# Prompt attention moved in among the steps of the sample attention, in one hybrid decoder layer

## The chip, the cores and the metric

The kernel runs on one core of a Trainium2 chip. The metric is device microseconds (us) of one execution, as the median of several runs. TensorE (PE) does the matrix products and the transposes, VectorE (DVE) and ScalarE (ACT) the elementwise work and the copies out of PSUM, GpSimd (POOL) some elementwise work and the indirect loads, SyncE (SP) issues most loads. Every engine works through its own instructions in the order in which they were written.

## What is computed

One decoder layer runs on 1024 prompt tokens and on 64 sample tokens (8 sequences of 8 tokens, each with 4096 cached tokens in pages of 128). Two feed-forward blocks stand around a middle part: an input projection, then attention over a latent of 256 numbers per token (8 heads, plus a rotated key of 32 numbers) beside a causal depthwise convolution of width 31, then one output projection over both. Cut to the two attentions:

```python
def attend_prompt(q_abs, q_pe, c_kv, k_pe):          # causal, blocks of 128 queries
    s = (einsum('bthc,bsc->bhts', qa_b, c_kv) + einsum('bthr,bsr->bhts', qp_b, k_pe)) * SM_SCALE
    p = softmax(where(qpos[:, None] >= kpos[None, :], s, NEG_INF))
    return einsum('bhts,bsc->bthc', p, c_kv)

def attend_sample(q_abs, q_pe, c_kv, k_pe, cache_kv, cache_kr, page_table):
    c_past, r_past = cache_kv[page_table], cache_kr[page_table]     # 4096 cached tokens
    s = concatenate([scores against the cache, causal scores against the 8 new tokens])
    p = softmax(s)
    return p_past @ c_past + p_new @ c_kv

attn_out = einsum('bthc,chv->bthv', o_lat, w_uv)
x = x + concatenate([rms_norm(attn_out), rms_norm(conv_out)]) @ w_out
```

## The kernel before

The kernel writes its own instruction order. `Flow` (`fl`) is a planner with a clock of its own: `fl.spend(ns)` lets that many planned nanoseconds pass, and side jobs (the convolution, norms, delayed stores) are written out when they fall due. A generator that yields `None` has nothing to write now.

**Sample attention** is `mgen`, 32 steps of 1024 cached tokens. A step (`qk`, `trans`, `expo`, `pv`) forms scores from eight cached key pages (`kst` tiles of two pages, six tiles ahead, `KBUF`), evicts them on DVE into `Ssb`, takes exponentials, transposes 4 blocks, and five or six steps later multiplies them with the cached values (`cst` tiles, seven ahead, `CBUF`). `load_k` reads the key pages: three tiles in four through SP, with a page number loaded into a register first, and every fourth tile as an indirect load of POOL. `load_c` reads the values as indirect loads of POOL.

**The filler** is written between these steps. After each piece of `mgen` the loop at its end adds `FILL_RATE` (0.8) times the piece's planned time to `due`, and takes filler from the generator `fill` until `due` is spent; when the filler yields `None`, `due` is set to zero and the sample goes on alone. The filler is `w2` (projections for the convolution, each followed by a `conv_chunk` that DVE works off at `CONV_SHARE`), then `pprep`, which splits weights into high and low parts, forms the prompt's keys `kT_all` and values `V`, and copies the rotated key from `kr_dram` into `kT_all` by eight broadcast loads. Its last quarter waits until the convolution has been written out (`while conv: yield None`), since it uses the convolution's buffers for the query weights.

**Prompt attention** comes after the sample's: 16 units `(i, p)` of 256 queries (`i`) and two heads (`p`). `stage_a` projects the unit's queries (two times nine products in high and low parts) and rotates them (`qf`); `stage_b` forms scores, evicts them with mask and running minimum into `P`, and `soft` takes the exponentials and divides each row by its sum, half the rows on DVE and half on ACT; `stage_c` transposes `P` and multiplies with `V`. The stages of neighbouring units alternate. Then `anorm` normalises, and the output projection begins (`colmm("u", ...)` from `w_out`).

Of the kernel before, what the change touches and what calls it, by code (L numbers as in the profile page):

```python
# [89 lines left out]
FILL_RATE = 0.8  # L90
KV_RATE = 0.6
# [12 lines left out]
def body(ctx, tc, A):  # L104
# [36 lines left out]
    q_dram = dram.tile([128, 3, N], F32, name="q_dram")  # L141
    ck_dram = dram.tile([128, 2, N], F32, name="ck_dram")
# [873 lines left out]
    kT_rows = A["kT"].rearrange("n p c s -> (n p) (c s)")  # L1016
# [78 lines left out]
    for i, (u, c) in enumerate(seq):  # L1095
# [12 lines left out]
        if i == 7:  # L1108
            for idx, m, mul, j in ((kidx, 96, 96, 0), (cidx, 128, 64, 1)):
                dve.tensor_scalar(out=idx[:m], in0=idx[:m], scalar1=mul, scalar2=None, op0=ALU.mult)  # L1110
                tt(idx[:m], idx[:m], iota[:m, j:j + 1].to_broadcast([m, idx.shape[1]]), ALU.add)
# [164 lines left out]
    es_kv, es_q = ExitStack(), ExitStack()  # L1276
    kT, at_ = [], {}
# [6 lines left out]
    def pprep():  # L1284
# [5 lines left out]
        V = at_["V"] = op("Vp", 1).tile([128, 8, CD], F32, name="V")  # L1290
        with ExitStack() as es:
# [59 lines left out]
        op = opener(es_q)  # L1351
        wqp, qp = op("wqp", 1), op("qp", 2)
        wq = at_["wq"] = [wqp.tile([128, 3, H, 128], F32R, name=f"wq{i}") for i in range(2)]
        at_["tabs"] = load(wqp, "tabs")
        at_["qp"] = qp
        qblk[0] = [qp.tile([128, 3, 256], F32R, tag=f"q{k}", name=f"qb{k}") for k in range(2)]
        split(*(t[:, :, 0:2] for t in wq), w0)
        split(*qblk[0], q0)
        sts = []
        for j in range(1, 4):  # L1360
            st = qp.tile([128, 3, 2, 128], F32, name="wqst", **(dict(tag=f"q{j % 2}") if j < 3 else dict(tag="st", bufs=1)))
            sp.dma_start(st, A["wqb_all"][:, :, 2 * j:2 * j + 2])
            sts.append(st)
        yield from hold(5000.0)
        for j, st in enumerate(sts):
            split(wq[0][:, :, 2 * j + 2:2 * j + 4], wq[1][:, :, 2 * j + 2:2 * j + 4], st)
            yield from hold(1500.0)

    qblk = {}

    def load_qblk(i):
        qp = at_["qp"]
        st = qp.tile([128, 3, 256], F32, tag="st", name="qst", bufs=1)
# [306 lines left out]
    for d in stage_a(0):  # L1680
        fl.spend(d)
# [213 lines left out]
```

## Time and profile before

| | |
|---|---|
| median of 3 runs | 2361.21 us (2360.1 to 2368.52) |
| the profiled execution | 2358.99 us, its span 2357.2 us |
| busy share of PE, DVE, POOL, ACT | 92%, 67%, 45%, 36% |
| DMA | 392.69 MB, mean 167 GB/s |
| mean granted clock of PE | 0.967 |

The trace's clock starts with the span. The first key product of the sample attention stands at 906.4 us, the last transposes of the sample's output at 1278.4, the first product of the output projection at 1487.6. A time in a row is from the span's start; "idle" in square brackets is what the engine waited before the instruction and what ended the wait. One matrix product on 32-bit numbers that are not split into high and low parts has two records in the trace, so counts of the trace are twice those of the program for these.

### The profile page before, as it was taken

How to read it: one execution, taken by the hardware profiler on the slowest of the kernel's cores; microseconds unless marked ns; L12 is line 12 of the kernel's file. 1: busy time of each engine (PE TensorE's matmuls, PEld its weight loads, DVE VectorE, ACT ScalarE, POOL GpSimd, SP SyncE). 2: the span in 40 equal slices, each digit the busy share in tenths (PEclk: the TensorE clock that was granted, in tenths of full speed). 3: DMA queues.
4: the chain of work that ended last, by engine and by line, in shares of the span. 5: the costliest groups of instructions: out<-in, count | busy, mean ns of one | idle time of the engine just before them, and what ended most of it. 6: DMA issues, size and time to landing. Idle time of an engine off the chain costs nothing. (4 is left out here: it accounts for less than half of the span.)

```text
span 2357.2 us, 42356 instructions
## 1 busy us (share of the span) xinstructions
PE 2178.0 (92%) x15714; PEld 1999.7 (85%) x15714; DVE 1568.2 (67%) x3061; ACT 843.8 (36%) x1759; POOL 1063.3 (45%) x995
## 2 busy tenths in 40 slices
PE   6989999999999898997688999899799999999997
PEld 6989999999999796785455765799799999999996
DVE  7976666666565666996533776577866656766567
ACT  4332222234344421211233656543332222334343
POOL 3446676631134303675455322343456777411234
PEclk8999999999999998998888999999999999999998
DMA  4126676648654434888575000452166666458653
GB/s 147 51 82 212 203 228 200 210 144 291 225 193 161 128 124 133 227 244 234 169 225 157 14 1 18 139 194 92 61 195 209 212 219 211 131 194 285 210 170 122
DMA packets 252527, 392.69 MB, mean 167 GB/s; under 512 B 26912, under 2 KB 188064, under 8 KB 252192
## 3 DMA queue, kind: packets, MB, share of 16 engines
q1 hardware_dynamic: 153184, 261.23, 35.2%
q10 hardware_dynamic: 85824, 85.75, 10.6%
q0 software_dynamic: 13312, 43.00, 6.3%
q8 instruction: 124, 2.03, 0.4%
q14 instruction: 83, 0.68, 0.1%
HBM read 299.71 MB, written 90.19 MB: 165 GB/s over the span
## 5 line engine op out<-in xcount | busy, mean ns | idle before, releaser
L110 DVE TENSOR_TENSOR wh<-wst,wh 128x512 fp32r<-128x512 f32 x355 | 302.7, 861 | 281.6 <-ACT wh L116 280.7
L110 POOL TENSOR_TENSOR ts<-ts 128x272 f32<-128x272 f32 (+1 forms) x352 | 309.3, 879 | 314.4 <-DMA ts<-a_dram 197.7
L127 PE MATMUL gu<-h,wh 128*128 128x272 f32 x1248 | 361.9, 290 | 11.9 <-DVE m L110 9.8
L128 PE MATMUL gu<-h,wh 128*128 128x272 f32 x1248 | 361.0, 289 | 4.0 <-DVE h L110 4.0
L129 PE MATMUL gu<-h,wh 128*128 128x272 f32 x1248 | 360.9, 289 | 1.2 <-DVE wh L110 1.2
L116 ACT ACTIVATE wh<-wst 128x512 fp32r<-128x512 f32 x355 | 217.9, 624 | 398.7 <-PE d L129 167.2
L127 PE MATMUL d<-h,wh 128*128 128x272 f32 x1232 | 355.5, 289 | 0.0
L128 PE MATMUL d<-h,wh 128*128 128x272 f32 x1232 | 353.9, 287 | 0.0
L129 PE MATMUL d<-h,wh 128*128 128x272 f32 x1232 | 353.8, 287 | 0.0
L127 PE MATMUL gu<-t,wh 128*128 128x272 f32 x936 | 273.5, 292 | 18.3 <-DVE sg L110 11.5
L129 PE MATMUL gu<-t,wh 128*128 128x272 f32 x936 | 271.7, 290 | 3.0 <-DVE wh L110 3.0
L128 PE MATMUL gu<-t,wh 128*128 128x272 f32 x936 | 271.2, 290 | 2.7 <-DVE t L110 2.7
L127 PEld LDWEIGHTS gu<-h,wh 128*128 128x128 f32 x1248 | 235.8, 189 | 14.7 <-DVE m L110 12.4
L128 PEld LDWEIGHTS gu<-h,wh 128*128 128x128 f32 x1248 | 235.9, 189 | 4.7 <-DVE h L110 4.7
L129 PEld LDWEIGHTS gu<-h,wh 128*128 128x128 f32 x1248 | 235.7, 189 | 1.4 <-DVE wh L110 1.4
L127 PEld LDWEIGHTS d<-h,wh 128*128 128x128 f32 x1232 | 231.6, 188 | 0.4
L128 PEld LDWEIGHTS d<-h,wh 128*128 128x128 f32 x1232 | 231.6, 188 | 0.2
L129 PEld LDWEIGHTS d<-h,wh 128*128 128x128 f32 x1232 | 231.4, 188 | 0.0
L1416 POOL DMA_INDIRECT cst<-in_cN,c_rep x128 | 142.5, 1113 | 182.2 <-DVE qx L1141 83.5
L127 PEld LDWEIGHTS gu<-t,wh 128*128 128x128 f32 x936 | 177.7, 190 | 22.4 <-DVE sg L110 14.4
L127 PE MATMUL u<-h,w 128*128 128x364 f32 (+3 forms) x528 | 183.0, 347 | 2.0 <-ACT h L116 2.0
L129 PEld LDWEIGHTS gu<-t,wh 128*128 128x128 f32 x936 | 177.7, 190 | 3.2 <-DVE wh L110 3.2
(260 smaller groups left out, 4884.9 us busy)
## 6 DMA issues: line engine op xcount, KB each, us to landing
wst<-in_wgu SPq DMA_DIRECT2D x88, 512.0 KB
kst<-in_kT SPq DMA_DIRECT2D x192, 144.0 KB
t_dram<-ts ACTq DMA_DIRECT2D x44, 544.0 KB
ts<-in_wd SPq DMA_DIRECT2D x88, 256.0 KB
a_dram<-acc ACTq DMA_DIRECT2D x78, 272.0 KB
wst<-s_dram SPq DMA_DIRECT2D x40, 512.0 KB
ast<-t_dram SPq DMA_DIRECT2D x66, 272.0 KB
s_dram<-ts ACTq DMA_DIRECT2D x44, 384.0 KB
```

The source lines that it names most:

```text
L110: eng.tensor_tensor(out=out, in0=a, in1=b, op=op)
L116: act.activation(out=out, in_=a, func=AF.Copy, scale=scale)
L127: pe.matmul(out, ah, bh, start=first, stop=False)
L128: pe.matmul(out, ah, bl, start=False, stop=False)
L129: pe.matmul(out, al, bh, start=False, stop=last)
L1416: pool.indirect_dma_start(out=t.rearrange("p a c -> p (a c)"), out_offset=None, in_=A["cN"], in_offset=bass.IndirectOffsetOnAxis(ap=cidx[: ...
```

## The change

- `FILL_RATE` is 1.45 throughout, and the filler has a third part, `prompt()`: the prompt attention. Units of `i = 3` wait until the sample attention has ended; what is left of the filler is then written out alone.
- The queries of all heads are projected in `pprep`, in 16 pieces of 512 columns instead of 32 halves of units of 256, and stored to `qh_dram`; a unit loads its queries back through SP. `pprep` doesn't wait for the convolution any more.
- Units that finish before the sample attention's buffers are free store their output to `at_dram`; it is loaded into `at` later.
- Rows of `P` are not divided any more. The reciprocals of a unit's sums are spread (`rw`), transposed by two PE transposes, copied by ACT (`rb`), and multiplied into the unit's output as DVE evicts it.
- All key pages are loaded through SP.
- PSUM: sample scores have one bank (two before), sample outputs one (two), transposes two (one), the prompt's outputs one. `Ssb` has one buffer less.

```diff
-FILL_RATE = 0.8
-KV_RATE = 0.6
+FILL_RATE = 1.45
...
+    qh_dram = dram.tile([128, H, S], F32, name="qh_dram")
+    at_dram = dram.tile([128, 4, S], F32, name="at_dram")
...
-            if g % 4 == 3:
-                pool.indirect_dma_start(out=t[:, j].rearrange("p c s -> p (c s)"), out_offset=None, in_=kT_rows,
-                                        in_offset=bass.IndirectOffsetOnAxis(ap=kidx[:96, pi:pi + 1], axis=0))
-            else:
-                v = sp.value_load(kidx[96:97, pi:pi + 1], min_val=0, max_val=NPHYS - 1)
-                sp.dma_start(t[:, j], A["kT"][bass.ds(v, 1)].rearrange("a p c s -> (a p) c s"))
+            v = sp.value_load(kidx[0:1, pi:pi + 1], min_val=0, max_val=NPHYS - 1)
+            sp.dma_start(t[:, j], A["kT"][bass.ds(v, 1)].rearrange("a p c s -> (a p) c s"))
...
-                if s == 3:
-                    while conv:
-                        yield None
-                    yield from hold(6500.0)
-                    w0, q0 = (gp.tile([128, CW - 1 + S], F32, tag="gx", name="early")[:, :768] for _ in range(2))
-                    w0, q0 = w0.rearrange("p (k h c) -> p k h c", k=3, h=2), q0.rearrange("p (k c) -> p k c", k=3)
-                    sp.dma_start(w0, A["wqb_all"][:, :, 0:2])
-                    sp.dma_start(q0, q_dram[:, :, 0:256])
...
-        wq = at_["wq"] = [wqp.tile([128, 3, H, 128], F32R, name=f"wq{i}") for i in range(2)]
...
+                if s == 2:
+                    qst = [fetch_q(0), fetch_q(1)]
+                    wst = deque([fetch_wq(0), fetch_wq(1)])
...
+        for h_ in range(H):
+            w = nxt
+            if h_ + 2 < H:
+                wst.append(fetch_wq(h_ + 2))
+            for j in range(2):
+                if h_ == 0 and j == 1:
+                    for v in range(2):
+                        split(*cols(2 + v), qst[v])
+                c0 = j * 512
+                ps = bank("u")
+                for k in range(3):
+                    mm3(ps, [t[:, k] for t in w], [t[:, k, c0:c0 + 512] for t in qc], k == 0, k == 2)
+                if j == 0 and h_ + 1 < H:
+                    nxt = split_wq()
+                qf = qfp.tile([128, 512], F32, tag="qf", name="qf")
+                tt(qf, ps, tabs[:, c0:c0 + 512], ALU.mult)
+                qhs.append(later(1500.0, (qh_dram[:, h_, c0:c0 + 512], qf)))
+                fl.spend(2050.0)
+                yield 2050.0
...
+    def prompt():
+        op = opener(es_b)
+        qfp, ap_, tp, sm, pp = op("qfp2", 3), op("ap", 2), op("tpp", 3), op("smp", 4), op("pp", 6)
+        mask = load(op("mkp", 1), "mask")
+        V = at_kv["V"]
...
+                sp.dma_start(q, qh_dram[:, 2 * p:2 * p + 2, i * 256:i * 256 + 256])
...
+        def soft(P, L, mn, s_):
+            if L > 512:
+                tt(mn[:, 0:1], mn[:, 0:1], mn[:, 1:2], ALU.min)
+                yield 300.0
+            act.activation(out=P[:, :L], in_=P[:, :L], func=AF.Exp, scale=-1.0, bias=mn[:, 0:1], accum_out=s_)
+            yield 0.0
...
+            rs = sm.tile([128, 2, 2], F32, tag="rs", name="rs")
+            dve.reciprocal(out=rs.rearrange("p v e -> p (v e)"), in_=U[u]["sums"].rearrange("p v e -> p (v e)"))
+            wide = sm.tile([128, 2, 2, 64], F32, tag="rw", name="rw", bufs=2)
+            dve.tensor_copy(wide, rs.unsqueeze(3).to_broadcast([128, 2, 2, 64]))
+            rb = sm.tile([128, 256], F32, tag="rb", name="rb", bufs=2)
+
+            def spread_sums():
+                ps = bank("t")[:, :256]
+                for v in range(2):
+                    pe.transpose(ps[:, v * 128:v * 128 + 128], wide[:, v].rearrange("p e d -> p (e d)"), ident)
+                acopy(rb, ps)
...
+                if jj == 1:
+                    spread_sums()
+                    yield 220.0
...
+            if at_:
+                tt(at_[0][:, p, i * 256:i * 256 + 256], o, rb, ALU.mult)
+            else:
+                t = ap_.tile([128, 256], F32, tag="a", name="ato")
+                tt(t, o, rb, ALU.mult)
+                early[i, p] = later(1500.0, (at_dram[:, p, i * 256:i * 256 + 256], t))
...
+        for u in range(len(units) + 1):
+            if u < len(units) and units[u] == (3, 0):
+                while not at_:
+                    yield None
+                pq.append(opener(es_b)("pp4", 6))
...
     def filler():
         yield from w2()
         yield from pprep()
+        yield from prompt()
...
+    psum_kinds(s=(3,), o=(6,), t=(5, 0), po=(4,))
...
-    cp, sb, ptp, sm = op("cp", CBUF), op("sb", LAG + 2), op("ptp", 2), op("sm", 2)
+    cp, sb, ptp, sm = op("cp", CBUF), op("sb", LAG + 1), op("ptp", 2), op("sm", 2)
...
-            ps = bank("s")[:64, :NS]
+            ps = bank("t")[:64, :NS]
...
-        due += d * (KV_RATE if at_ else FILL_RATE)
+        due += d * FILL_RATE
...
-    if fill is not None:
-        for d in fill:
-            if d is None:
-                fl.spend(300.0)
...
+    at_.append(at)
+    psum_kinds(u=(1, 2, 3), t=(5, 0, 6))
...
+    for (i, p), done in early.items():
+        fl.wait(done)
+        sp.dma_start(at[:, p, i * 256:i * 256 + 256], at_dram[:, p, i * 256:i * 256 + 256])
...
-    def stage_a(u):
-        i, p = units[u]
-        U[u] = dict(q=[], P={}, pt={}, soft=[])
-        for e in range(2):
-            ps = bank("t")[:, :256]
-            for k in range(3):
-                mm3(ps, [t[:, k, 2 * p + e] for t in wq], [t[:, k] for t in qblk[i]], k == 0, k == 2)
-            qf = qp.tile([128, 256], F32, tag="qf", name="qf", bufs=4)
-            tt(qf, ps, tabs[:, i * 256:i * 256 + 256], ALU.mult)
-            U[u]["q"].append(qf)
-            yield 960.0
...
-        act.activation(out=P[:, :L], in_=P[:, :L], func=AF.Exp, scale=-1.0, bias=mn[:, 0:1], accum_out=s_[:, 0:1])
-        yield 900.0 +  0.4 * L
-        dve.reciprocal(out=rs[:, 0:1], in_=s_[:, 0:1])
-        if v:
-            yield 300.0
-            acopy(P[:, :L], P[:, :L], rs[:, 0:1])
-        else:
-            dve.tensor_scalar(out=P[:, :L], in0=P[:, :L], scalar1=rs[:, 0:1], scalar2=None, op0=ALU.mult)
...
-        acopy(at[:, p, i * 256:i * 256 + 256], o)
...
+    for c in late_an:
+        anorm(c)
+    sample_out()
+    if fill is not None:
+        for d in fill:
+            if d is None:
+                fl.spend(300.0)

```

On PE, near the end of `pprep` in the kernel before: `kst` rows are key products of the sample, `Ssb` its transposes, `cst` its value products, `st` rows belong to norms.

```order
L1434 MATMUL s<-kst,qx 64x256 x6
L207 MATMUL st<-dg,ones 128x364
L1473 MATMUL t<-c_ident,Ssb 128x128 x4
L1434 MATMUL s<-kst,qx 64x256 x6
L1491 MATMUL o<-cst,spt 64x256 x8
```

On PE in the changed kernel, four steps before the last key products: scores (`kT_all,qf`) and transposes (`P`, `rw`) of the prompt's first units.

```order
L1596 MATMUL s<-kst,qx 64x256 x6
L1430 MATMUL u<-kT_all,qf_15303 128x128
L1430 MATMUL u<-kT_all,qf_15303 128x256
L1430 MATMUL u<-kT_all,qf_15303 128x128
L1430 MATMUL u<-kT_all,qf_15303 128x256
L1430 MATMUL u<-kT_all,qf_15306 128x128
L1469 MATMUL t<-c_ident,P 128x128 x3
L1655 MATMUL o<-cst,spt 64x256 x8
L1469 MATMUL t<-c_ident,P 128x128 x3
L198 MATMUL st<-ones,ss 91x1 x4
L1430 MATMUL u<-kT_all,qf_15306 128x256
L1459 MATMUL t<-c_ident,rw 128x128 x2
```

Prompt units now stand between the sample's products from step 28 on (of 0 to 31); units 0 to 7 are over when the sample ends.

On POOL, the last loads of values in the kernel before; `th` and `zc` rows are the norm behind the convolution.

```order
L1425 MEMSET mn 128x5
L1426 MEMSET sums 128x5
L1032 DMA kst<-in_kT,c_prep 96x384 x2
L1416 DMA cst<-in_cN,c_rep 128x512 x4
L1032 DMA kst<-in_kT,c_prep 96x384 x2
L1416 DMA cst<-in_cN,c_rep 128x512 x4
L1032 DMA kst<-in_kT,c_prep 96x384 x2
L1416 DMA cst<-in_cN,c_rep 128x512 x25
L110 TENSOR_TENSOR th<-th,zc 128x364
```

On POOL in the changed kernel, the same place:

```order
L1578 DMA cst<-in_cN,c_rep 128x512 x12
L109 TENSOR_TENSOR th<-th,zc 128x364
L109 TENSOR_TENSOR zc<-zc,th 128x364
L109 TENSOR_TENSOR th<-th,zc 128x364
L109 TENSOR_TENSOR zc<-zc,th 128x364
L1578 DMA cst<-in_cN,c_rep 128x512 x4
L109 TENSOR_TENSOR th<-th,zc 128x364
L109 TENSOR_TENSOR zc<-zc,th 128x364
L1587 MEMSET mn 128x5
L1588 MEMSET sums 128x5
```

The key loads are gone from POOL, and of its last 37 loads of values all now stand among or behind 36 elementwise instructions of the norm, which stood behind the last load before.

On SP, around the broadcast loads of the rotated key, before:

```order
L1036 DMA kst<-in_kT 96x384
L1337 DMA kT_all<-kr_dram 64x1x1024 x2
L1035 TENSOR_LOAD c_prep
L1035 ISA x2
L1036 ISA
L1036 DMA kst<-in_kT 96x384
```

And in the changed kernel:

```order
L1032 DMA kst<-in_kT 96x384
L1339 DMA kT_all<-kr_dram 64x1x1024 x4
L1031 TENSOR_LOAD c_prep
L1031 ISA x2
L1032 ISA
L1032 DMA kst<-in_kT 96x384
```

The eight broadcast loads stood in groups of 2, 2, 3 and 1 among key pages before; now there are two groups of four, with eight key pages between them, and all key pages of that time are behind them on SP.

## Rows read from the trace of the kernel before

**Rows 1.** The page: engines' busy time, share and instructions; DMA share in 40 slices.

```profile
PE 2178.0 (92%) x15714; PEld 1999.7 (85%) x15714; DVE 1568.2 (67%) x3061; ACT 843.8 (36%) x1759; POOL 1063.3 (45%) x995
...
DMA  4126676648654434888575000452166666458653
```

**Rows 2.** Stretches: length, busy PE, PEld, DVE, ACT, POOL, PE clock, DMA share, GB/s.

```profile
906.40:1081.30 174.90, 165.63 (x1168) 129.54 (x1169) 154.87 (x286) 31.94 (x73) 110.28 (x105) 0.96 0.80 222
1081.30:1211.30 130.00, 86.15 (x544) 56.72 (x540) 61.78 (x122) 30.21 (x75) 62.38 (x60) 0.80 0.65 192
1211.30:1278.80 67.50, 57.17 (x362) 33.44 (x361) 22.12 (x64) 26.15 (x63) 43.40 (x48) 0.92 0.77 231
1278.80:1358.00 79.20, 77.52 (x494) 58.41 (x493) 57.63 (x214) 51.27 (x151) 28.63 (x30) 0.96 0.07 23
1358.00:1487.60 129.60, 117.51 (x704) 75.17 (x702) 88.99 (x299) 80.46 (x163) 28.26 (x29) 0.97 0.03 9
```

**Rows 3.** PE in order of time, one projection unit: start, us, what.

```profile
1005.71 0.43 PE L127 MATMUL u<-h,w 128*128 128x364 f32 x1
...
1009.80 0.63 PE L1473 MATMUL t<-c_ident,Ssb 128*128 128x128 f32 x4
```

**Rows 4.** DVE in order of time, the convolution.

```profile
1014.14 1.27 DVE L113 SCALAR_TENSOR_TENSOR zc<-gx,c_wdw,zc 128x1024 f32<-128x1024 f32 x1
```

**Rows 5.** PE in order of time, key products that waited for their pages.

```profile
1111.67 0.79 PE L1434 MATMUL s<-kst,qx 96*64 96x256 f32 x2 [12.58 <-DMA kst<-in_kT]
...
1135.62 0.70 PE L1434 MATMUL s<-kst,qx 96*64 96x256 f32 x2 [5.61 <-DMA kst<-in_kT,c_prep]
...
1165.52 1.51 PE L1434 MATMUL s<-kst,qx 96*64 96x256 f32 x4 [11.88 <-DMA kst<-in_kT]
...
1192.67 1.21 PE L1434 MATMUL s<-kst,qx 96*64 96x256 f32 x4 [10.89 <-DMA kst<-in_kT]
```

**Rows 6.** SP in order of time, and its waits from 1060 to 1290 us.

```profile
1114.49 3.75 SPq L1036 DMA_DIRECT2D kst<-in_kT  x4
...
1130.14 8.50 SPq L1337 DMA_DIRECT2D kT_all<-kr_dram  x2
1139.97 27.37 SPq L1036 DMA_DIRECT2D kst<-in_kT  x10
...
SPq L1036 <- DMA kT_all<-kr_dram: 15.5, 4, 6.5
```

**Rows 7.** Groups of PE in the third stretch: busy, mean ns, idle before.

```profile
L127 PE MATMUL u<-ck,uk 128*128 128x256 f32 x8 | 2.6, 321 | 0.0
...
L129 PE MATMUL u<-uv,ck 128*128 128x512 f32 x5 | 2.0, 395 | 0.0
```

**Rows 8.** Groups of POOL: loads of values; norm from 1285 us.

```profile
L1416 POOL DMA_INDIRECT cst<-in_cN,c_rep x127 | 140.0, 1102 | 98.7 <-PE o L1491 69.0 <-issue 21.0 <-PE s L1434 3.2
...
L110 POOL TENSOR_TENSOR ss<-ss,sq 128x364 f32<-128x364 f32 x15 | 15.3, 1019 | 40.1 <-ACT sq L242 39.6 <-DVE s L1622 0.2
```

**Rows 9.** Prompt stage: PE in time; groups of PE and DVE, two stretches.

```profile
1359.15 0.36 PE L127 MATMUL t<-qb,wq 128*128 128x256 f32 x1
...
1360.31 0.60 PE L1643 MATMUL t<-c_ident,P 128*128 128x128 f32 x4
...
L127 PE MATMUL t<-qb,wq 128*128 128x256 f32 x60 | 21.8, 363 | 0.0
...
L127 PE MATMUL t<-qb,wq 128*128 128x256 f32 x36 | 11.9, 332 | 0.0
...
L1643 PE MATMUL t<-c_ident,P 128*128 128x128 f32 x208 | 29.6, 278 | 8.9 <-DVE pt L1650 3.7 <-DVE s L110 2.3 <-DVE v L113 1.8
...
L1627 DVE TENSOR_SCALAR P<-P,s 128x640 f32<-128x640 f32 x7 | 5.9, 839 | 0.2
L1627 DVE TENSOR_SCALAR P<-P,s 128x896 f32<-128x896 f32 x8 | 5.8, 719 | 0.3
L110 DVE TENSOR_TENSOR qf<-t,c_tabs 128x256 f32<-128x256 f32 x12 | 5.0, 418 | 2.5 <-PE t L129 2.3
```

More of the change, by code (lines that the diff above doesn't have):

```diff
@@ L1108, in body @@
         if i == 7:
-            for idx, m, mul, j in ((kidx, 96, 96, 0), (cidx, 128, 64, 1)):
-                dve.tensor_scalar(out=idx[:m], in0=idx[:m], scalar1=mul, scalar2=None, op0=ALU.mult)
-                tt(idx[:m], idx[:m], iota[:m, j:j + 1].to_broadcast([m, idx.shape[1]]), ALU.add)
+            dve.tensor_scalar(out=cidx, in0=cidx, scalar1=64, scalar2=None, op0=ALU.mult)
+            tt(cidx, cidx, iota[:, 1:2].to_broadcast([128, cidx.shape[1]]), ALU.add)
             for _ in range(KBUF):
@@ L1364, in pprep @@
-        yield from hold(5000.0)
[L1365 to L1373, printed above, removed]
-        sp.dma_start(st, q_dram[:, :, i * 256:i * 256 + 256])
-        yield 6000.0
-        qblk[i] = [qp.tile([128, 3, 256], F32R, tag=f"q{k}", name=f"qb{k}") for k in range(2)]
-        split(qblk[i][0], qblk[i][1], st)
+                if s == 2:
+                    qst = [fetch_q(0), fetch_q(1)]
+                    wst = deque([fetch_wq(0), fetch_wq(1)])
@@ new lines, in pprep, with split_wq @@
+        op = opener(es_p)
+        qc = [op(f"qc{k}", 1).tile([128, 3, S], F32R, name=f"qc{k}") for k in range(2)]
+        wqp, qfp = op("wqp", 2), op("qfp", 2)
+        def split_wq():
+            w = [wqp.tile([128, 3, 128], F32R, tag=f"wq{k}", name=f"wq{k}") for k in range(2)]
+            split(*w, wst.popleft())
+            return w
+        cols = lambda j: [t[:, :, j * 256:j * 256 + 256] for t in qc]
+        nxt = split_wq()
+        for j in range(2):
+            split(*cols(j), qst[j])
@@ L1423, in qk @@
             B[b] = dict(mn=sm.tile([128, 5], F32, tag="mn", name="mn", bufs=3),
-                        sums=sm.tile([128, 5], F32, tag="sums", name="sums", bufs=3), o=bank("o")[:, :KVR])
+                        sums=sm.tile([128, 5], F32, tag="sums", name="sums", bufs=3))
             pool.memset(B[b]["mn"], BIG)
@@ L1480, in pv @@
         d = B[b]
+        if pg == 0:
+            d["o"] = bank("o")[:, :KVR]
         pt, o = d.pop(("pt", pg)), d["o"]
@@ L1496, in pv @@
             pe.matmul(o[0:64], ptn, cx, start=False, stop=True)
-            return fl.add(finish(b))
+            fin = finish(b)
+            next(fin)
+            return fl.add(fin, 6000.0)
     def finish(b):
@@ L1673, in body @@
-    an = []
-    def anorm(c):
-        c0, n = CH[c]
-        nm = Norm(lambda k: at[:, k, c0:c0 + n], 4, CD, n)
-        an.append(fl.add(nm.whole(900.0, pool, g_oa, keep=nm.src, lag=5000.0, lag2=5000.0)))
-    for d in stage_a(0):
-        fl.spend(d)
-    for u in range(len(units) + 1):
-        if u == 1:
-            sample_out()
-        gb = stage_b(u) if u < len(units) else iter(())
-        other = deque()
-        cost = 0.0
-        if u + 1 < len(units):
-            other.append(stage_a(u + 1))
-            cost += 1920.0
-        if u:
-            other.append(stage_c(u - 1))
-            cost += (units[u - 1][0] + 1) * 1720.0
-        done = 0.0
-        for k in range(4):
-            d = next(gb, None)
-            if d is not None:
-                fl.spend(d)
-            while other and (done < cost * (k + 1) / 4 or k == 3):
-                d = next(other[0], None)
-                if d is None:
-                    other.popleft()
-                    continue
-                done += d
-                fl.spend(d)
-                other.rotate(-1)
-        if u and units[u - 1][1] == 3 and units[u - 1][0]:
-            anorm(units[u - 1][0] - 1)
+    for c in late_an:
+        anorm(c)
```

206 lines of the change are left out of this document (117 added, 89 removed).

## The prediction

> **What bounds the kernel now.** I read the page first. PE is busy 92% of the span and DVE 67%; one slice group in the DMA line falls to 0, the others stand between 2 and 9 [rows 1]. So any gain must come out of PE's idle time or out of PE work that disappears. Next I cut the part from the sample's first key product to the output projection, 906.4 to 1487.6 us or 581.2 us, into five stretches with one row each [rows 2]: A, steps 0 to 18, with the projections of the convolution as filler (174.9 us); B, steps 19 to 27, with the prompt's keys and values as filler (130.0); C, steps 28 to 31 and the sample's last value products (67.5); D, the prompt attention, in the rows 79.2 and 129.6, together 208.8. A row's first number behind the length is PE's busy time, so PE stands still for 9.3 us in A, 43.9 in B, 10.3 in C, 1.7 and 12.1 in D: 77.3 us in all. B holds more than half of it, at a mean clock of 0.80. In D the transfers nearly rest (share 0.07 and 0.03), while A is at 0.80, with DVE busy 154.87 of its 174.9 us, so A has no slack on three resources at once.
>
> Then I asked what PE waits for in B: key products that stand 12.58, 5.61, 11.88 and 10.89 us until their pages land, 41.0 of the 43.9 [rows 5]. SP's own sequence shows why. Four pages with nothing between them take 3.75 us, 0.94 each; two broadcast loads of `kT_all` take 8.50 us, and the ten pages behind them 27.37, or 2.74 each [rows 6]. SP waits 15.5 us on `kT_all` alone [rows 6]. In D the waits that remain are short ones, 8.9 us before the transposes of `P`, released by DVE's copies and evictions [rows 9].
>
> **What that means for the change.** In PE's own work it saves almost nothing: the prompt attention is as long among the steps as behind them. It can give back only part of the 77 us, of which B has 44, plus what the low clock costs there. I take the stretches in turn, each against its old length.
>
> **A: the same filler, in clumps.** A projection unit of 24 products of 364 columns takes 1009.80 − 1005.71 = 4.09 us, 0.468 ns a column [rows 3]. In A's part of the order there are 17 such units before and after, 69.5 us; the rest of PE's 165.6 us, 96.1, is the sample's own. If each of the first five steps, which have no value products yet, takes half of a full one (an estimate), a full step takes 96.1/16.5 = 5.8. At rate 1.45 the units stand in steps 0 to 3, 7 to 10 and 13 to 15, and eight steps have none. In those, the single bank of scores counts: the next key products wait for DVE to evict the last ones, which can stand behind a convolution instruction of 1.27 us [rows 4]. At most 1.3 us in eight steps is 10; half of that, **+5**, is my value. Lower end −5 (half of A's idle time is covered), upper end +15 (all of it, and 5 for transfers that are no longer spread evenly).
>
> **B: more filler, but every page on SP.** B now gets all that is left of `pprep`. Keys are 96 products of 256 columns, 11.5 us; values 48 of 512, 11.5; queries 144 of 512, 34.5. With nine steps at 5.8, 52.4, PE has 110 us of work. The SP side: before, 54 of B's 72 pages were SP's, 54 × 0.94 = 50.8, so the broadcast loads and what they hold up account for the other 79.2 us. Now all 72 are SP's: 67.7 + 79.2 = 147 us. POOL's own 62 us of 130 [rows 2] don't bound it, so what POOL is relieved of gains nothing here. The two groups of four broadcast loads have only eight pages between them, and PE has at most six tiles (a step and a half) in hand. SP's 147 is longer than PE's 110, so I take 147, **+17**. Lower end: the pages flow past the broadcasts and PE sets it, 113, −17. Upper end: each pair of broadcasts costs what the seen one did, 8.50 plus 27.37 − 9.4, or 26.5; four are 106, and with 67.7 that is 174, +44.
> By the Trainium skill (DMA: Bandwidth & Descriptors, "Why a DMA increments its semaphore by 16 and not by 1") a load from SP runs on the largest number of engines up to 16 that divides the slowest dimension of both sides, and the `kT_all` loads have a 2 there. At 222 GB/s for a share of 0.80 [rows 2], two of 16 engines carry 35 GB/s, so 256 KB take 7.6 us and eight loads 60 (an estimate by that page); B would be 128 and the sum 19 us lower, 2307. No row here shows the number of engines. The rows charge more than that to the broadcasts, and I stay with the rows.
>
> **C: half of the prompt attention moves in.** Units 0 to 7 (`i` = 0 and 1) stand between the sample's products from step 28 on and are over when it ends. PE's 57.2 us there lose the rest of the old filler, three lines like the first of [rows 7] (24 products of 256 columns, 2.9) and 13 products of 512 (3.1): 51.2. The units bring the first row of D, 77.5, less its 20 query halves. One half is 1360.31 − 1359.15 = 1.16 us, and 60 products are 20 halves of three [rows 9], so 23.2 go: 54.3. Some 4 us of that (sample output, the first of `i` = 2) I leave behind: 50. The spread sums add 16 transposes at 0.15 [rows 9]: 2.4. Together 104, **+36**. The other path is POOL: its last 37 value loads at (140.0 + 21.0)/127 = 1.27 us and, in order among them, 36 norm instructions of 1.02 [rows 8]: 84 us. A value load queued behind such an instruction holds PE's value products, and all of PE behind them. It is shorter than PE's 104, so it sets only the lower end, +16. Upper end: the two do not overlap, and 20 us of PE's waits stand in between, +57.
>
> **D: only `i` = 2 and 3.** PE's 117.5 us of the second row lose 12 query halves, 36 products of the kind in [rows 9], 13.9; they gain 2.4 of transposes and the 4 left behind: 110. DVE loses 11.7 us of division of `P` [rows 9] and its share of rotations; per unit it gains a reciprocal, a spreading copy and the last product, each priced by its rotation of 256 columns, 0.42 us [rows 9], 10 us for eight units. So DVE is not much lighter, ACT is, and I let PE's idle 12.1 fall by half: 116. Against 208.8 that is **−93**. Lower end 105 (no idle time, nothing left behind), −104; upper 125 (all of the idle time and 3 more), −84.
>
> **Edits that I cost at nothing.** The queries' way through DRAM: the stores are delayed by the planner and lie beside a DMA that is at 0.65 to 0.77 there; 16 reloads stand two units ahead on SP. If one is late, SP holds the key pages queued behind it, at 0.5 us for its issue and more for its wait; that price is in B's and C's upper ends. The 7 stores and loads of `at_dram` are needed only by norms in D, where the DMA rests. The old 32 halves of 1.16 and the 16 new pieces of 2.16 differ by 2.5 us. One buffer less of `Ssb` is covered as long as the lag of five steps holds.
>
> **The sum** is 5 + 17 + 36 − 93 = −35 against the profiled 2358.99: 2324.0. The median of the runs lies 2.2 above the profiled one, so I say **2326**.
>
> **Rivals.**
> *More gain (0.20).* PE sets every stretch: A 0, B −17, C +28, D −100, in all −89, which gives 2272. For it: with 110 us of products in B each step lasts twice as long as its own work, and pages have time. Against it: the pages stood behind two loads for 27 us, longer than any one step.
> *No change (0.14).* The idle time only moves: A +10, B +35, C +48, D −88, in all +5, 2366. For it: POOL's order in C and SP's in B are both tighter than before, and PE takes its instructions in order, so a late page stops the prompt's products too. Against it: PE's work at 104 covers POOL's 84.
> *Slower (0.12).* SP becomes the bound of the whole sample. Of 256 pages 12 are loaded ahead, 244 go through SP one by one. In my forecast they take A, B and about 44 us of C, 371 us, 1.52 each. With 60 us of C behind the last page and 116 for D, the old 581 are reached at (581 − 176)/244 = 1.66 us a page; above that the kernel is slower. If a third of them cost the 2.74 of [rows 6], the mean is 1.93, and 471 + 176 = 647, or +66: 2427. Against it: the undisturbed 0.94.
> *The units do not overlap.* That is excluded in the order (they do stand there), not in time; its time is C's upper end, and it lies inside the forecast's range.
>
> **How the numbers follow.** The forecast's own case has 0.54, with 2285 to 2355 as its range. A measurement of this kernel can tell about 0.5%, 12 us, from no change. Faster by more: 0.51 of the forecast's 0.54, the 0.20, and 0.02 of the third, 0.73. Slower by more: the 0.12 and 0.03 of the others, 0.15. Within: 0.12. The range leaves out the slower case, half of which begins above 2376, and the lower part of the larger gain: 2270 to 2376.
>
> **What would show it.** In the profile of the changed kernel: A, 180 us, with short waits of key products on DVE in steps without filler; B about 147, with PE still waiting 30 us for `kst` pages, in two blocks behind the two groups of `kT_all`, and SP's page spacing above 2 us only there; C about 104, PE over 90% busy, the waits for `cst` under 10 us; D about 116, with a unit of `i` = 2 some 12 us apart and of `i` = 3 some 16. The prediction is wrong low if SP's pages stand at 1.66 us or more over the whole sample, wrong high if the waits for `kst` are gone from B.

## The result: slower by 1.6%, and the profile after

The changed kernel takes 2401.58 us in the median of 4 runs (2397.24 to 2404.93); the kernel before took 2364.09 (2360.1 to 2368.52, 4 runs). The ratio is 1.0157, with a 95% interval of 1.0128 to 1.0186. I had said 2326, within 2270 to 2376.

The windows of the changed kernel, cut at the same places of the program as [rows 2] (first key product; first key products of step 19 and of step 28; last transposes of the sample's output; output projection). Columns: length, busy PE, PEld, DVE, ACT, POOL, PE clock, DMA share, GB/s.

```profile
908.00:1116.80 208.80, 182.56 (x1170) 133.04 (x1169) 157.40 (x288) 31.61 (x72) 69.91 (x67) 0.91 0.72 197
1116.80:1285.80 169.00, 120.90 (x733) 85.05 (x734) 87.65 (x175) 46.93 (x109) 48.47 (x45) 0.86 0.59 177
1285.80:1413.00 127.20, 101.99 (x638) 61.19 (x634) 57.92 (x203) 56.49 (x170) 70.33 (x75) 0.91 0.51 149
1413.00:1533.30 120.30, 103.14 (x616) 63.87 (x616) 73.80 (x259) 64.24 (x146) 20.16 (x21) 0.99 0.07 23
```

| us | before | forecast | after | forecast of the step | measured |
|---|---|---|---|---|---|
| A | 174.9 | 180 | 208.8 | +5 | +33.9 |
| B | 130.0 | 147 | 169.0 | +17 | +39.0 |
| C | 67.5 | 104 | 127.2 | +36 | +59.7 |
| D | 208.8 | 116 | 120.3 | −93 | −88.5 |
| sum | 581.2 | 547 | 625.3 | −35 | +44.1 |

D came out near its forecast; A, B and C each cost 22 to 29 us more than foreseen. PE was not given more to do: summed over the stretches it is busy 504.0 us before and 508.6 after, while its idle time went from 77.2 to 116.7 us. (Each row's busy time times its clock, summed, estimates PE's work in time at full clock: 469 us for [rows 2], 165.63 × 0.96 + 86.15 × 0.80 + 57.17 × 0.92 + 77.52 × 0.96 + 117.51 × 0.97, and 465 for the four rows above. A row's clock is a mean over its waits too, so a few us between such sums say nothing. What lies on top, waits and low clock, went by this from 112 to 160 us.) Outside the four stretches the two spans differ by 4 us the other way; that was not followed. So the question is which waits the new order made.

**In A** PE's idle time grew by 17 us and its busy time by another 17 (182.56 against 165.63), at a clock of 0.91 instead of 0.96. The idle time stands before key products. The first view below groups PE's instructions in A of the changed kernel (busy, mean ns, idle before); the second is SP in order of time; the third has two PE waits at the end of A; the fourth has two short stretches of A, with the columns of the rows above.

```profile
L1596 PE MATMUL s<-kst,qx 96*64 96x256 f32 x458 | 74.5, 425 | 24.7 <-DMA kst<-in_kT 22.7 <-DVE mn L1602 1.7 <-issue 0.2
```

```profile
930.28 26.87 SPq L1032 DMA_DIRECT2D kst<-in_kT  x24
957.25 0.37 SPq L313 DMA_DIRECT2D wst<-in_w_in  x1
958.45 26.77 SPq L1032 DMA_DIRECT2D kst<-in_kT  x24
```

```profile
1102.22 0.69 PE L1596 MATMUL s<-kst,qx 96*64 96x256 f32 x2 [4.04 <-DMA kst<-in_kT]
...
1110.15 0.66 PE L1596 MATMUL s<-kst,qx 96*64 96x256 f32 x1 [4.08 <-DMA kst<-in_kT]
```

```profile
943.00:978.00 35.00, 24.89 (x122) 13.22 (x118) 15.43 (x26) 4.22 (x11) 5.04 (x5) 0.77 0.67 176
1094.00:1112.00 18.00, 8.11 (x31) 3.79 (x32) 4.91 (x11) 1.68 (x4) 5.56 (x5) 0.72 1.02 291
```

Pages follow each other on SP at 26.87/24 = 1.12 us, so the eight pages of a step need 9.0 us, against 5.8 us of the sample's own products (the prediction's estimate). In steps 4 to 7, from 942 to 978 us, which have no filler, PE runs ahead of them. SP itself waits only 0.8 us between 930 and 985 us, so this is its own pace. PE's waits for pages are 8.4 us there, and with them goes the clock, 0.77 in the first of the two stretches.

The row's 22.7 us of waits for pages have two more places: 5.6 us around 1034 us and 8.1 from 1098 to 1110 us. In the last one the DMA engines are full (share 1.02) behind the loads of the weights `suk` and `suv`, which SP issues from 1094.60 us on. The kernel before has a wait of 12.58 us [rows 5] behind the same loads (SP issues them there from 1090.85 us on), but in B. Some 8 us of A's loss have thus moved in from B and are no new cost. The single bank of scores, which I had priced, is the 1.7.

**In B** PE waits twice, and neither time for a page. PE, then ACT, then SP, in order of time:

```profile
1165.78 0.58 PE L126 MATMUL u<-ck,uk 128*128 128x256 f32 x1 [23.71 <-ACT V L115]
...
1193.87 1.11 PE L1660 MATMUL o<-cx,ptn 64*64 64x256 f32 x2 [17.43 <-ACT ptn L115]
```

```profile
1164.48 0.63 ACT L115 ACTIVATE ck<-ckst 128x512 fp32r<-128x512 f32 x1 [25.79 <-DMA ckst<-ck_dram]
...
1192.47 0.63 ACT L115 ACTIVATE ck<-ckst 128x512 fp32r<-128x512 f32 x1 [18.66 <-DMA ckst<-ck_dram]
```

```profile
1128.14 8.27 SPq L1339 DMA_DIRECT2D kT_all<-kr_dram  x4
1137.76 23.24 SPq L1032 DMA_DIRECT2D kst<-in_kT  x8
1161.10 0.57 SPq L1313 DMA_DIRECT2D ckst<-ck_dram  x1
1161.72 4.85 SPq L1339 DMA_DIRECT2D kT_all<-kr_dram  x4
1167.89 7.50 SPq L1032 DMA_DIRECT2D kst<-in_kT  x4
1175.50 1.12 SPq L1313 DMA_DIRECT2D ckst<-ck_dram  x1
```

Four broadcast loads are issued; the eight pages behind them take 23.24 us, and only then comes the load of `ckst`, the next block of latents for the prompt's keys. ACT stands 25.79 us before the split of that block, with the eviction of `V` behind it, and PE behind the eviction. The second load of `ckst` is issued at 1175.50 us, and ACT gets to split its block only at 1192.47: this one was issued behind four more broadcasts and was then 17 us on its way. The DMA view of 1128 to 1170 us has 40 slices of about 1 us; its rows are the share of the engines in tenths and the rate:

```profile
DMA  7894731111699992111543454115111167211111
GB/s 231 212 312 175 221 105 31 43 55 51 147 281 221 234 242 78 55 51 51 174 151 109 153 176 156 55 51 166 62 52 49 48 169 208 68 51 51 55 66 51
```

In the slices of lowest share, where I take only broadcasts to be left, a tenth of the engines moves 51 GB/s. At that rate the eight loads of 256 KB take 41 us together.
The Trainium skill (DMA: Bandwidth & Descriptors, "Why a DMA increments its semaphore by 16 and not by 1") says that such a load, with a 2 in its slowest dimension, runs on two engines of 16; a tenth in the row agrees with that. My estimate from the mean rate per engine had been 60 us for the eight; the row gives 41.

**In C** PE's busy time is 102.0 us, as forecast (104). The 25 us on top are waits of PE, 14.3 of them for copies of transposed `P`; PE's groups from 1285.8 to 1413 us, those with idle time before them and the value products:

```profile
L1430 PE MATMUL u<-kT_all,qf 128*128 128x512 f32 (+3 forms) x80 | 32.5, 511 | 6.9 <-DVE s L1431 5.4 <-DMA qf<-qh_dram 1.5
L1655 PE MATMUL o<-cst,spt 128*64 128x256 f32 x163 | 21.6, 407 | 0.0
L1469 PE MATMUL t<-c_ident,P 128*128 128x128 f32 x80 | 13.9, 301 | 14.3 <-DVE pt L1476 14.3
...
L1648 PE MATMUL t<-c_ident,Sn 64*64 64x64 f32 x3 | 0.7, 233 | 3.7 <-ACT pt L115 3.0 <-DVE v L109 0.7
```

The value products (`cst`) do not wait in C any more, so POOL's order, which I had feared there, did not decide it.

### The profile page after: what moved, and what is told of

It reads as the page before. It is cut to its first block, busy times and chain, and to the rows that moved or that the text cites. A ratio compares the mean times of both kernels' runs of the same rounds, so it can differ in the third digit from the quotient of the medians.

```text
span 2397.5 us, 42496 instructions
## 1 busy us (share of the span) xinstructions
PE 2185.7 (91%) x15602; PEld 1992.6 (83%) x15602; DVE 1555.2 (65%) x2999; ACT 822.9 (34%) x1731; POOL 997.8 (42%) x931
## 5 line engine op out<-in xcount | busy, mean ns | idle before, releaser
L115 ACT ACTIVATE wh<-wst 128x512 fp32r<-128x512 f32 x355 | 218.2, 625 | 402.8 <-PE d L128 166.2
L1578 POOL DMA_INDIRECT cst<-in_cN,c_rep x128 | 151.2, 1181 | 394.5 <-PE o L1655 264.0
L126 PE MATMUL gu<-t,wh 128*128 128x272 f32 x936 | 275.5, 294 | 16.5 <-DVE sg L109 13.8
L126 PEld LDWEIGHTS gu<-t,wh 128*128 128x128 f32 x936 | 179.1, 191 | 21.2 <-DVE sg L109 17.5
```

Source lines behind the costliest of these rows:

```text
L115: act.activation(out=out, in_=a, func=AF.Copy, scale=scale)
L126: pe.matmul(out, ah, bh, start=first, stop=False)
L1578: pool.indirect_dma_start(out=t.rearrange("p a c -> p (a c)"), out_offset=None, in_=A["cN"], in_offset=bass.IndirectOffsetOnAxis(ap=cidx[: ...
```

## Experiments

Stretches are from each kernel's profiled run. The kernel before took 2368 us beside e1_pool to e4_fill, 2356 beside e5_late, e6_actpt, e7_rate and b1_kt, and 2359 beside the rest (2364 in the runs of the result), so whole times are compared by their ratio to before. Between kernels of different groups the ratios and the sums of stretches differ by up to some 20 us; where in the kernel that comes from was not followed, so such comparisons rest on the stretches, each of one execution.

| kernel | A | B | C | D | sum | ratio to before (95%) |
|---|---|---|---|---|---|---|
| before | 174.9 | 130.0 | 67.5 | 208.8 | 581.2 | 1 |
| after | 208.8 | 169.0 | 127.2 | 120.3 | 625.3 | 1.0157 (1.0128 to 1.0186) |
| e1_pool | 196.0 | 166.2 | 125.3 | 122.2 | 609.7 | 1.0089 (1.0058 to 1.0120) |
| e2_kt | 209.7 | 134.5 | 130.2 | 122.8 | 597.2 | 0.9994 (0.9974 to 1.0013) |
| e3_both | 194.7 | 136.3 | 126.9 | 122.4 | 580.3 | 0.9936 (0.9913 to 0.9960) |
| e4_fill | 183.2 | 133.1 | 98.9 | 193.8 | 609.0 | 1.0058 (1.0039 to 1.0077) |
| e10_actq | 211.7 | 154.0 | 129.1 | 122.8 | 617.6 | 1.0134 (1.0111 to 1.0158) |
| e5_late | 198.0 | 135.5 | 78.3 | 186.0 | 597.8 | 1.0080 (1.0051 to 1.0109) |
| e6_actpt | 196.1 | 129.7 | 119.0 | 116.3 | 561.2 | 0.9945 (0.9920 to 0.9970) |
| e7_rate | 180.6 | 135.1 | 99.6 | 149.2 | 564.4 | 0.9922 (0.9901 to 0.9943) |
| e8_best | 180.3 | 131.1 | 97.6 | 145.8 | 554.8 | 0.9888 (0.9867 to 0.9909) |
| e9_rate11 | 179.0 | 124.0 | 90.8 | 163.5 | 557.3 | 0.9899 (0.9880 to 0.9918) |
| b1_kt | 176.0 | 98.7 | 68.3 | 206.2 | 549.2 | 0.9889 (0.9864 to 0.9913) |
| b2_scale | 175.5 | 102.2 | 72.7 | 205.3 | 555.8 | 0.9892 (0.9873 to 0.9912) |

### Pages on SP alone: e1_pool

```diff
+            if g % 4 == 3:
+                pool.indirect_dma_start(out=t[:, j]..., in_=kT_rows, in_offset=...kidx[:96, pi:pi + 1])
+            else:
...
+                v = sp.value_load(kidx[96:97, pi:pi + 1], min_val=0, max_val=NPHYS - 1)
```

> The changed kernel with one thing undone: every fourth tile of key pages is an indirect load of POOL again. Theory: in the changed kernel's stretch A (208.8 us, 174.9 before) SP sets the pace in the steps without filler, since its pages stand 1.12 us apart there (24 in 26.87) and eight are 9.0 us against 5.3 of products; with six of eight pages a step needs 6.7. So A falls by 15 to 25 us, B by 0 to 10 (its idle time is 41 us behind two late ckst loads, which this does not touch), and the time to about 2378 (2368 to 2388). Rival, that the clumped filler alone costs A (bursts of transfers, not their issue): A stays within 5 us of 208.8 and the time at 2400.

A fell by 12.8 us, to 196.0, B by 2.8. SP's spacing is the same, 20.23/18 = 1.12 us, but a step now needs six pages of it; SP in order of time:

```profile
926.66 20.23 SPq L1037 DMA_DIRECT2D kst<-in_kT  x18
```

So SP's issue is a part of A's loss, 13 of 34, a little below what I had expected. The page waits in A fell from 22.7 to 18.3 us only, and 11.24 of these are the wait behind the weights' loads, which this edit does not touch; the clock is 0.93 instead of 0.91, and the rest of the gain is shorter busy time, 173.65 instead of 182.56.

### The filler's rate alone: e4_fill

```diff
-FILL_RATE = 1.45
+FILL_RATE = 0.8
```

> The changed kernel with FILL_RATE 0.8 as before; prompt units start later, more of them follow the sample. Theory: A has filler in every step again, SP has time for its pages there, and A falls by 20 to 30 us to some 182, with all pages still on SP; but work moves from B and C to behind the sample, where D grows. B keeps its wait behind the broadcasts and overlaps less work with it. In all 2375 (2355 to 2400). Rival, that SP's issue limits A whatever the order of the filler: A stays above 200.

A fell by 25.6 us with every page still on SP. The clumps of filler are thus needed for the loss: with filler in every step the page waits in A are 7.3 us. A part of the 25.6 is a shift, since the waits around the weights' loads, 9.3 us here, stand in B again, as before. Both edits attack the same wait from its two sides. B fell too, to 133.1: units and queries are later there, and PE is busy only 94.6 us of it, at a clock of 0.79; its two long waits behind the broadcasts, 14.20 and 13.61 us, stay, as expected. Of the 90 us that A, B and C gained D took back 73.5: 193.8.

### The broadcasts' shape: e2_kt, b1_kt, e10_actq

```diff
-                        sp.dma_start(kT[4 * s + p][64:128], kr_dram[:, 0:S].unsqueeze(0).to_broadcast([2, RD, S]))
+                        for r in (64, 96):
+                            sp.dma_start(kT[4 * s + p][r:r + 32], kr_dram[:, 0:S])
```

> The changed kernel with each of the eight broadcast loads of kT_all replaced by two loads of 32 rows of 1024, the same bytes. Theory: the broadcasts run on few DMA engines and hold SP and the ckst loads queued behind them, which ACT, and PE behind ACT, wait for (23.7 and 17.4 us of PE in B). With loads that spread they are over in a few us: PE's 41 us go, the clock stays up, B falls from 165.7 by 35 to 50 to some 120, and the time to about 2358 (2350 to 2368). Rival, that key pages and other loads on one queue of SP hold ckst whatever the broadcasts' shape: B stays over 150 and the time over 2390.

B fell by 34.5 us, just under the expected 35 to 50; A, C and D together rose by 6.4, and the time, 2369.7, lies 2 us above its range. B of e2_kt, to be held against the second row of the result:

```profile
1119.50:1254.00 134.50, 119.60 (x734) 84.06 (x734) 88.27 (x177) 46.86 (x109) 48.21 (x44) 0.94 0.76 224
```

PE's busy time is the same 120, the clock 0.94 instead of 0.86, and 33 us of waits are gone.

> The kernel before with the eight broadcast loads as two loads of 32 rows each, as in e2_kt. Theory: B of the kernel before has 41 us of waits for pages, of which the first 12.6 lie ahead of the broadcasts (behind the weights' loads at full DMA) and stay; the other 28 go: B 130 to 102, the time lower by 20 to 30 us, ratio 0.988 to 0.992. Rival, that in the kernel before the pages of POOL and the smaller groups of broadcasts already hide them: less than 8 us.

The same edit in the kernel before takes 31.3 us off its B, 1.1% of the whole. No other kernel of the study is faster against before by more than the noise, and this edit has nothing to do with the change. B and C of it:

```profile
1083.00:1181.70 98.70, 78.66 (x544) 52.27 (x540) 61.82 (x122) 30.29 (x75) 63.64 (x60) 0.91 0.94 252
1181.70:1250.00 68.30, 57.75 (x363) 33.71 (x362) 22.00 (x64) 26.13 (x63) 44.03 (x48) 0.92 0.75 229
```

PE's idle time in B fell from 43.9 to 20.0 us, and the DMA share is 0.94, so transfers are now close to setting B; that was not tried. The first wait, 12.58 in [rows 5], stands there at 11.57, as expected.

```diff
-                        sp.dma_start(kT[4 * s + p][64:128], kr_dram...to_broadcast([2, RD, S]))
+                        act.dma_start(kT[4 * s + p][64:128], kr_dram...to_broadcast([2, RD, S]))
```

> The changed kernel with its eight broadcast loads unchanged in shape but issued by ACT, so that SP's queue holds key pages and ckst loads only. It tells the two halves of the mechanism of e2_kt apart. In the changed kernel from 1128 to 1170 us the transfers stand at 31 to 55 GB/s in most slices, against 250 and more in others. If it is SP's own order that holds pages and ckst behind the broadcasts, B falls by 25 to 35 us as in e2_kt, and the time to about 2370. If it is the few engines that carry the broadcasts, which pages need as well, whoever issues them, B falls by less than 12 us; between these, both count.

B fell by 15.0, between the two cases: SP's order is one half, and a load that few engines carry stays in the way whoever issues it. That fits the two loads of `ckst` above, one issued late and one long on its way. The sum of the stretches is 7.7 us lower, and the ratio is not told apart from that of the changed kernel. The half is not clean, because ACT now stands itself, once 8.38 us, behind its own issues (ACT and its queue in order of time):

```profile
1144.19 4.07 ACTq L1339 DMA_DIRECT2D kT_all<-kr_dram  x1
1148.31 0.77 ACT L115 ACTIVATE kT_all<-u 64x256 f32<-64x256 f32 x2 [8.38 <-issue]
```

### Both repairs: e3_both

> The changed kernel with both edits: a quarter of the key pages on POOL, and the broadcasts as loads of 32 rows. Theory: the two costs lie in different stretches (A and B) and add up: 20 and 43 us off 2401, so 2338 (2325 to 2355), below the kernel before. Rival, that both cure the same shortage of SP: the sum is not reached and the time is within 8 us of the better of the two alone.

The gains add up: A 14.1, B 32.7, the sum of the stretches 45.0 us lower, against 15.6 and 28.1 of the two edits alone. The time, 2354.2, came out at the upper end of what I had expected, since A gave 14 us and not 20, and B 33 and not 43; the ratio, 0.9936, is below 1 all the same.

### Is it worth moving the units in? e5_late

```diff
+        while not at_:
+            yield None
         pq = [pp]
         load_q(0)
```

> e3_both with the prompt units held back until the sample attention has ended; queries, scaling at the end, pages and rates as in e3_both. It tells what moving the units in is worth by itself. In e3_both the stretches C and D take 132.7 and 116.7, 249.4. Theory: the units among the sample's last steps gain next to nothing, since PE is the engine that both need and the mixed order adds waits: C near the 77.7 of before less its old filler, 72, and D 198.6 less 37 of query halves plus some transposes, 170: 242, so the time is 0 to 12 us lower than e3_both. Rival, that the units do fill idle time: C and D together take 258 or more and the time is 10 us or more above e3_both.

My theory fell. C shrinks by 48.6 us, but D grows by 63.6; the ratio is 1.0080 against 0.9936 of e3_both. So the units among the sample's last steps do fill time: 15 us of it by C and D, 18 by all four stretches and by the times themselves (2372.5 and 2354.2), 34 by the ratios, which stem from two groups of runs. I had taken D as before less 37 us of query halves, 170; it is 186.0. D of e5_late, and below it that of b2_scale, which has the queries' products in D and the same scaling at the end; then a group of PE's instructions in D of e5_late:

```profile
1316.90:1502.90 186.00, 159.76 (x911) 99.27 (x910) 116.07 (x402) 102.99 (x268) 40.69 (x43) 0.96 0.08 26
```

```profile
1256.90:1462.20 205.30, 195.34 (x1226) 135.92 (x1226) 137.41 (x464) 108.75 (x282) 56.09 (x58) 0.98 0.05 14
```

```profile
L1476 PE MATMUL t<-c_ident,P 128*128 128x128 f32 x288 | 42.4, 282 | 14.9 <-DVE pt L1483 11.3 <-ACT pt L115 2.0 <-ACT P L1448 1.1
```

PE's busy time is 36 us shorter, the stretch only 19: PE stands still 26 us instead of 10, and 14.9 of these before transposes of `P` (3.4 in b2_scale). I take it that the query projections had been what PE did while DVE and ACT worked on the scores, and that they leave waits behind when taken out. The two kernels also differ in their PSUM banks, so this is argued and not shown.

### Copies of P on ACT: e6_actpt

```diff
-                    if e or jj % 2:
+                    if True:
```

> e3_both with all copies of transposed P out of PSUM on ACT (half of those of the first head were on DVE). In stretch C PE waits 20.7 us for such copies of DVE, and DVE 35.2 us for scores of PE: DVE's copy stands behind an eviction of scores that PE has not formed yet. Theory: with the copies on ACT that ring is broken, C falls by 10 to 25 us, and the time to about 2338. D, where ACT then carries more, changes by less than 5. Rival, that the waits only change their name (ACT's copies stand behind exponentials): C within 5 us of 132.7.

C fell by 7.9 us, between the 10 of the theory and the 5 of its rival, and D by 6.1. In C the wait for copies of DVE, 13.2 us in e3_both, is gone, and 2.9 us for those of ACT stand in its place. PE's groups in C of e6_actpt:

```profile
L1437 PE MATMUL u<-kT_all,qf 128*128 128x512 f32 (+3 forms) x80 | 30.0, 477 | 7.3 <-DVE s L1438 6.4 <-DMA qf<-qh_dram 0.9
...
L1476 PE MATMUL t<-c_ident,P 128*128 128x128 f32 x80 | 13.0, 287 | 2.9 <-ACT pt L115 2.9
...
L1466 PE MATMUL t<-c_ident,rw 128*128 128x128 f32 x16 | 3.1, 277 | 3.7 <-DVE rw L1460 3.7
```

The 3.7 us before `rw` are new, a wait on DVE; PE's idle time in C fell from 24.9 to 17.5 us. B, which the edit does not touch, was 6.6 us shorter in this run, and the ratio to before is not distinguishable from that of e3_both: the gain is seen in its stretch, not in the whole time.

### The rate by part: e7_rate, e8_best, e9_rate11

```diff
+    rate = [0.8]
+
     def filler():
         yield from w2()
+        rate[0] = FILL_RATE
...
-        due += d * FILL_RATE
+        due += d * rate[0]
```

> e3_both with rate 0.8 while the filler is the convolution's projections (stretch A) and 1.45 afterwards. Theory: A's remaining 20 us over before (194.7 against 174.9) are the steps that have no filler, in which pages come too slowly; spread again, A returns to 175 to 180, B and C stay, and the time falls by 14 to 20 us to about 2337. Rival, that the single bank of scores and the fewer buffers cost A in any order: A stays above 188.

A is 180.6, close to before, so the rival fell: the single bank of scores does not keep A long, though its waits grew to 7.1 us there, from 1.7 in the changed kernel. But C did not stay: five units lie in it instead of eight, and what C gains (27.3) D takes (26.8). The sum is 15.9 us lower. By length this is A's 14 us; by PE's idle time, 65.8 us against 81.0 in e3_both, A gave 9 of it and C 14, while B took 7 (the wait behind the weights' loads, 7.49 us in A of e3_both, stands in B here with 10.16). So the edit pays, but not in A alone, as its theory had it; the ratio does not tell it from e3_both.

> e3_both with the edits of e6_actpt and e7_rate together. Theory: they act in different stretches (e7 took 14 us off A and left units for D; e6 took 10 off C, 7 off B, 4 off D), so 10 to 16 us below e7_rate: stretches A to D together 545 to 552 against 564 and 561 with one of them, 2320 to 2328 in units of a before of 2356; ratio 0.985 to 0.988. That is level with b1_kt (0.989, stretches 549): moving the units in is then worth no more than not moving them. Rival, that both act on the same waits of PE for copies (the end of C): no better than 558.

Sum 554.8, 3 us above the expected range; ratio 0.9888: below e3_both with disjoint intervals, level with b1_kt, whose edit it contains. Here are its four stretches:

```profile
908.00:1088.30 180.30, 168.56 (x1168) 131.09 (x1169) 155.41 (x286) 31.95 (x73) 110.82 (x105) 0.95 0.76 215
1088.30:1219.40 131.10, 108.67 (x660) 74.52 (x657) 77.22 (x152) 42.59 (x100) 64.19 (x61) 0.90 0.81 232
1219.40:1317.00 97.60, 88.00 (x564) 57.07 (x563) 46.84 (x157) 44.46 (x136) 67.54 (x73) 0.97 0.61 189
1317.00:1462.80 145.80, 129.03 (x763) 80.52 (x762) 83.34 (x298) 90.60 (x220) 30.83 (x32) 0.98 0.10 32
```

Busy time at full clock is about 470 us, as before and after; waits and low clock are 85 us, against 160 in the changed kernel.

> e8_best with 1.1 instead of 1.45 behind the convolution's projections: fewer prompt units among the sample's last steps, more behind it. Theory: in B the PE work for nine steps shrinks from about 110 to 100 and B becomes bound by its transfers; C shrinks and D grows by what is moved; the sum within 6 us of e8_best, since PE's work is the same and the waits that are left are short. Rival, that mixing costs PE more than it hides: e9_rate11 is 8 us or more faster.

Sum 557.3: B and C 13.9 us shorter, D 17.7 longer. Between these two rates it does not matter where PE's work stands, within 3 us.

### Scaling at the end alone: b2_scale

```diff
-        dve.reciprocal(out=rs[:, 0:1], in_=s_[:, 0:1])
...
-            dve.tensor_scalar(out=P[:, :L], in0=P[:, :L], scalar1=rs[:, 0:1], scalar2=None, op0=ALU.mult)
...
-        acopy(at[:, p, i * 256:i * 256 + 256], o)
+        tt(at[:, p, i * 256:i * 256 + 256], o, rb, ALU.mult)
```

> b1_kt with one part of the change alone: rows of P are not divided, the unit's output is scaled as DVE evicts it (a reciprocal and a spreading copy on DVE, two transposes on PE, a copy on ACT for each unit). Theory: D of b1_kt has PE busy 183 of 197 us, so the lighter DVE and ACT take 2 to 7 us of PE's 14 us of waits, and 16 units of two transposes of 0.15 us add 5: between 3 us slower and 4 us faster than b1_kt. Rival, that the division's latency before the transposes of P sets the pace of a unit: 8 us or more faster.

D is 205.3 against 206.2, the ratios are the same. DVE is 10 us and ACT 23 us lighter in D, PE 3 us busier, and its waits fell from 13.8 to 10.0 us. This part of the change is worth nothing by itself.

## Why the prediction was wrong

**The step that failed is the overlap.** "In PE's own work it saves almost nothing", and 77 us of idle time is all that can be had: that held (504.0 and 508.6 us busy). The sum then let PE's idle time fall to about 57 us, each forecast length less PE's time in it: 14 in A, 37 in B, none in C, 6 in D. It rose to 116.7: 26.2, 48.1, 25.2 and 17.2. PE's work moved as forecast, but the waits did not lie beside it.

**A (+5, measured +33.9): the supply of pages was put at nothing.** I counted the same 17 units and priced the steps without filler by the one bank of scores, half of 10 us. That wait is 1.7 us. For B I had 0.94 us a page and "every page on SP" in hand, and did not ask how long eight pages take in a step of 5.8 us. At 1.12 us it is 9.0. e1_pool and e4_fill show both halves: fewer pages on SP give 13 us, filler in every step 26, some of it a shift to B. The other thing that I overlooked is the wait behind the weights' loads, which the faster filler brings forward from B into A, 8 us. The 0.94 was misread, too. The last of the four pages of [rows 6] is

```profile
1117.92 0.32 SPq L1036 DMA_DIRECT2D kst<-in_kT  x1
```

and a row's time runs from its first start to its last end, so 3.75 us hold three distances and one issue: (3.75 − 0.32)/3 = 1.14 us a page.

**B (+17, measured +39.0): the queue right; victim, size and overlap wrong.** I let SP's queue behind the broadcasts set B, 147 us, with PE's 110 beside it, and expected 30 us of waits for pages. The queue was held, but the waits were for two loads of `ckst` behind the broadcasts, through ACT, and 41 us long. The 79.2 us that I had charged to the broadcasts and what they hold up were too much: without them B is 31.3 us shorter in the kernel before (b1_kt) and 34.5 in the changed one (e2_kt). And these 34.5 did not pass beside PE's work, they lay on top of the 134.5 that B takes without them. The upper end I gave, +44, holds the value.

**C (+36, measured +59.7): the work right, the overlap wrong.** 104 us of PE work was right to 2 us. That PE would never wait in C was an assumption: units and sample steps alternate there so tightly that PE waits for DVE's copies and DVE for PE's scores (35.2 us of DVE in C). e6_actpt removes 8 us of 25 by taking the copies off DVE. What the other waits in C hang on was not tried. POOL's 84 us, the lower end, played no part; the upper end, +57 for 20 us of waits on top, was passed by 3.

**D (−93, measured −88.5): the length near, by two errors that cancel.** PE is busy 103.1 us and not 110, and idle 17.2 and not 6. e5_late points the same way: without the query products a unit is not shorter by their whole length.

**The rivals.** "Slower" named SP as the bound and 1.66 us a page as the point from which it decides. From 909.6 to 1326.9 us the 244 pages stand 1.71 us apart on average, so the point was passed; but not since SP could not go faster (1.12 where nothing holds it). It was held behind the broadcasts in B, and otherwise waited for PE to free its tiles, some 25 us in A and 30 in B. Its point was right, its mechanism holds for the steps without filler only, and its 1.93 us a page counted the held pages twice, since the 1.52 already contains them. "No change" came nearest by stretch: its B (+35) and D (−88) are within 4 us and its C (+48) within 12; it missed A, and its ground for C, POOL's order, is not what happened. "More gain" needed pages that flow past the broadcasts; e3_both, where they do, is at 0.9936, a sixth of the 89 us.

**What stays open.** How much of the 20 us that A of e3_both lies above before is the clumps' doing: e7_rate has 180.6, but a wait of A stands in B there. The last 17 us of waits in C are named in its rows but not taken apart.

## To carry to other kernels

When work is moved into a stretch that another engine or queue feeds, ask in each step without that work how fast its supply comes, and look at everything that stands behind a slow transfer on its queue, not only at the transfer that waits now. Work that leaves a stretch takes its cover with it: the stretch becomes shorter by less than the work. And where idle time has one cause, remove that first: two loads in place of one broadcast gave 1.1% to the kernel before (b1_kt, 0.9889). The change with the faults mended that were found, this edit among them, gives as much (e8_best, 0.9888), so moving the units in gave nothing beyond it.

## What the hardware showed that I had not expected

A broadcast load of [2, 32, 1024] from DRAM ran at 51 GB/s, a tenth of the DMA engines, where the first slices of the same view, with pages and values, stand at 175 to 312; the same bytes as two loads of 32 rows left no such trough (B of e2_kt at 224 GB/s on average). Such a load also held up the engine that issues it: the eight pages behind four of them took 23.24 us on SP, and ACT stood up to 8.38 us when it issued them. And SP's pages, each with a page number read into a register first, stand about 1.15 us apart wherever nothing holds them: (26.87 − 0.32)/23 in the changed kernel, (3.75 − 0.32)/3 = 1.14 in [rows 6].
